# A hybrid encoder layer: the first norm's weight moved behind the transposes, all token tiles loaded first, some roots on ScalarE, the last token tile in two column halves

## The chip, the cores and the metric

The kernel runs on one core of a Trainium2 chip. The core has five engines with their own instruction streams: TensorE (PE; its weight loads are listed as PEld), VectorE (DVE), ScalarE (ACT), GpSimd (POOL) and SyncE (SP), which here issues the transfers between device memory and on-chip memory. Engines wait for each other by semaphores. Matrix products are written to PSUM, eight banks of 128 x 512 float32; everything else lives in SBUF, with 128 partitions. The metric is the time of one execution on the device in microseconds (us); lower is better.

## The reference, cut to what matters

One layer of an encoder trunk over 1024 tokens of width 1024, in float32. Each of its three sub-layers normalises its input, computes, normalises its output and adds it to the residual:

```python
def _rms_norm(x, gain):
    y = x * lax.rsqrt(jnp.mean(x * x, axis=-1, keepdims=True) + EPS)
    return y * gain

h = _rms_norm(x, g_mix_pre)
proj = h @ w_in                       # (1024, 1024) @ (1024, 2832)
...                                   # windowed attention and two-way gated DeltaNet
x = x + _rms_norm(mix @ w_out, g_mix_post)
...                                   # cross-attention into 256 memory tokens
x = x + _rms_norm(c, g_cross_post)
f = _swiglu(_rms_norm(x, g_ffn_pre), w_gate_up, w_down)
return x + _rms_norm(f, g_ffn_post)
```

The change touches the first norm (`g_mix_pre`) and the last one (`g_ffn_post`), at the two ends of the kernel.

## The kernel before, in words

Tokens go in eight tiles of 128 rows. A product in full precision is made of three products of rounded parts: each operand is split into a high part (a cast, usually on ScalarE, line 103) and a low part (the difference, usually on VectorE, line 104) by `split`, and `gemm_b` (line 260) issues high x high, high x low and low x high for each of the eight slices k of the inner dimension.

The instructions are written in Python and then placed by a planner: within each engine they are ordered by a priority, which follows the program's order, as its simulated clock makes them ready. `tc.high_priority(300)` in `load_w` moves weight loads and their splits 300 places up, and `tc.issue_after(i)` puts an instruction behind `i` on the same engine. Each engine then runs its stream strictly in that order. Buffers of one tag are reused in turn: an instruction that writes a buffer waits for the last reader of what was in it before. All transfers are issued by SyncE, in the planner's order too.

The start (lines 201 to 232). Six token tiles of `x` are loaded (line 205), and after the first of them `gmix`, the first norm's weight, which is spread to all 128 partitions (512 KB), and the identity matrix for transposes. Tiles 6 and 7 take over the buffers of tiles 0 and 1 (line 217). For each tile: ScalarE squares it and sums the squares (line 220), GpSimd makes the inverse root in two operations (`rstd_of`, lines 160 and 161), VectorE multiplies the tile by the root and by `gmix` in one operation (line 223), TensorE turns its eight 128 x 128 blocks into two PSUM tiles (line 228), and each of these is split into the high and low part of the turned activations `hT` (lines 103 and 104). Four tiles make a half `hf`. The first weights, two columns blocks of 128, are loaded behind tiles 1 and 3 (line 293), and their products with both halves follow (line 298): 96 matmuls of 128 x 512. Next come the products with `wabr` (line 314), a small weight that is zeroed (line 306) and filled (307, 308). In between, a small table of gains and convolution taps (`rows`) is turned (line 242), two masks are cast (246, 247), and `nega` is an exponential of a parameter (252).

The end (lines 1709 to 1783). The down projection of the feed-forward part is done by seven block products. The last of them runs over four token tiles t; for each, the activations come in two pieces of 6 and 5 slices (line 1763), are split, and 33 matmuls add to the PSUM tile X[t] (line 1768). After that, for token tile r = 4 + t: the sum `zv` (line 1775), its sum of squares on ScalarE (`sq_of`, line 1690), the gain `gp` (1777), the inverse root on GpSimd (`rstd_at`, lines 1705 and 1706), and for each column half the scaling together with the residual (1780) and the store (1781). The other half's sum of squares, in `sq[:, 1]`, has been made before the loop. `first_half` finishes tiles 2 and 3 within the same loop.

Of the kernel before, what the change touches and what calls it, by code (L numbers as in the profile page):

```python
# [76 lines left out]
def tile_hybrid_block(  # L77
# [16 lines left out]
    def f32(ap):  # L94
        return ap.bitcast(F32)
# [61 lines left out]
    def rstd_of(rs, ss, n, eps):  # L157

        w = ss.shape[-1]
        nc.gpsimd.tensor_scalar(rs, ss, n, eps, ALU.mult, ALU.add)  # L160
        nc.gpsimd.tensor_tensor(rs, rs, mhalf[:, :w], ALU.pow)


    gain_at = {"cross": 60, "mem": 60 + KT, "ffn": 60 + 2 * KT}
# [44 lines left out]
    hT = []  # L209
    for hf in range(2):  # L210
        hi = hx.tile([P, KT, HALF], F32R, name=f"hhi{hf}")
        lo = hx.tile([P, KT, HALF], F32R, name=f"hlo{hf}")
        for j in range(4):
            t = 4 * hf + j
            xt = xts[t] if t < 6 else t1.tile([P, D], F32, tag="xt", name="xt", bufs=6)
            if t >= 6:
                nc.sync.dma_start(xt, x[t * P:(t + 1) * P, :])
            junk = t1.tile([P, D], F32, tag="junk", name="junk", bufs=1)
            ss = t1.tile([P, 1], F32, tag="ss", name="ss", bufs=4)
            nc.scalar.activation(junk, xt, AF.Square, accum_out=ss)  # L220
            rs = t1.tile([P, 1], F32, tag="rs", name="rs", bufs=4)
            rstd_of(rs, ss, 1.0 / D, EPS)
            nc.vector.scalar_tensor_tensor(xt, xt, rs, gmix, ALU.mult, ALU.mult)
            for kq in range(2):
                pt = small()
                for k in range(4):
                    c = (4 * kq + k) * P
                    nc.tensor.transpose(pt[:, k * P:(k + 1) * P], xt[:, c:c + P], ident)
# [16 lines left out]
    nc.sync.dma_start(C, consts[:, C0:C1])  # L245
    nc.vector.tensor_copy(mU_r, cm["mU"])
    nc.vector.tensor_copy(mL_r, cm["mL"])
# [4 lines left out]
    nc.scalar.activation(nega, prm[:, 0:8], AF.Exp)  # L252
    nc.vector.tensor_scalar(nega, nega, -1.0, None, ALU.mult)
# [51 lines left out]
    wabr = tb.tile([P, KT, P], F32R, tag="V", name="wabr", bufs=1)  # L305
    nc.vector.tensor_scalar(wabr, hT[0][0].bitcast(F32)[:, :, 0:P], 0.0, None, ALU.mult)
    nc.vector.tensor_copy(wabr[:, :, 0:16], wab)
# [1380 lines left out]
    def sq_of(src, t, ch):  # L1688
        jk = tp_.tile([P, 512], F32, tag="jk", name="jk", bufs=1)
        nc.scalar.activation(jk, src, AF.Square, accum_out=sq[:, ch, t:t + 1])  # L1690

# [62 lines left out]
    for t in range(4):  # L1754
        nc.vector.tensor_tensor(za[:, t], za[:, t], X[t], ALU.add)
        sq_of(za[:, t], 4 + t, 1)

    for t in range(4):
        tt = slice(t * P, (t + 1) * P)
        for k0, n in ((0, 6), (6, 5)):  # L1760
            with tc.high_priority(AHEAD):
# [3 lines left out]
                split(ah, al, ar)  # L1765
            for k in range(n):
                for i, (a, w) in enumerate(((ah, t4h), (ah, t4l), (al, t4h))):
                    nc.tensor.matmul(X[t], a[:, k], w[:, k0 + k], start=False, stop=(k0 + k == NB - 1 and i == 2),  # L1768
                                     skip_group_check=True)
        if t < 2:  # L1770
# [3 lines left out]
        nc.vector.tensor_tensor(za[:, t], za[:, t], gp[:, 512:], ALU.mult)  # L1774
        nc.vector.tensor_tensor(zv[:, t], zv[:, t], X[t], ALU.add)
        sq_of(zv[:, t], r, 0)
        nc.vector.tensor_tensor(zv[:, t], zv[:, t], gp[:, 0:512], ALU.mult)
        rs = rstd_at(r)
        for z, o_ in ((za, 512), (zv, 0)):
            nc.vector.scalar_tensor_tensor(z[:, t], z[:, t], rs, xr[:, o_:o_ + 512], ALU.mult, ALU.add)  # L1780
            nc.sync.dma_start(out[there(r), o_:o_ + 512], z[:, t])
    LB.close()
# [31 lines left out]
```

## Time and profile before

| | |
|---|---|
| time, median of 3 runs | 1532.86 us (1529.66 to 1533.37) |
| the profiled execution's own time | 1531.94 us |
| its span, first to last instruction | 1530.2 us |
| TensorE busy | 1477.9 us, 97% of the span |
| VectorE, ScalarE, GpSimd busy | 1111.5, 743.0, 399.9 us |
| mean granted TensorE clock | 0.992 |
| HBM read and written | 179.41 MB, 75.27 MB |

The profile is one execution, recorded by the hardware profiler. A timeline row gives the start in us from the span's start, the duration in us, the engine, the line of the kernel (which can be a helper's), the operation, what it writes and reads by the program's names, and how many like it are merged (x8). In brackets stands the engine's idle time before it and what ended it. A row of the groups by line gives the count, then busy us and mean ns of one, then idle time and its releasers. A row of the stretches gives, for a stretch of time, its length and the busy time and number of instructions of PE, PEld, DVE, ACT and POOL, then the granted clock, the busy share of the DMA engines and GB/s. The chain of waits follows the work that ended last, from step to step, with start and duration; SPq, DVEq and the like are an engine's sequencer. Matmuls are pipelined: a recorded 0.39 us per matmul stands for a start every 0.23 us.

### The profile page before, as it was taken

The page shows a single profiled execution, that of the slowest core. Times are in us where ns is not written, and L with a number is a line of the kernel's source. Part 1 is how long each engine was busy: PE and PEld are TensorE (multiplying, and loading weights), DVE is VectorE, ACT ScalarE, POOL GpSimd, SP SyncE. Part 2 cuts the span into 40 slices and gives each one's busy share as a digit, 9 for nine tenths or more (in the row PEclk, how much of TensorE's full clock was granted, in tenths as well). Part 3 has the DMA queues.
Part 4 walks back from the last instruction along what each step waited for, and adds up shares of the span by engine and source line. Part 5 has one row for each costly group of instructions (what it writes and reads, how often), then busy time and mean ns, then how long its engine had stood idle before and what let it go on. Part 6 is the DMA issues. An engine that isn't in the chain of part 4 may idle for free.

```text
span 1530.2 us, 21184 instructions
## 1 busy us (share of the span) xinstructions
PE 1477.9 (97%) x7403; PEld 1241.1 (81%) x7403; DVE 1111.5 (73%) x1790; ACT 743.0 (49%) x1516; POOL 399.9 (26%) x404
## 2 busy tenths in 40 slices
PE   6999999998999899999999899999999999999997
PEld 5888888887989778887788687888888888888786
DVE  6868999787889865538567778686877554696665
ACT  5678821457557664455544673322233332454532
POOL 3020221311336203242201532353434332000021
PEclk9999999999999999999999999999999999999999
DMA  6235575857987674457724733343433333953255
GB/s 206 77 105 152 140 198 145 224 166 204 315 283 223 202 276 155 152 161 257 235 97 173 232 124 117 113 149 107 156 124 104 103 103 111 325 204 97 103 177 167
DMA packets 272360, 258.70 MB, mean 169 GB/s; under 512 B 34792, under 2 KB 204669, under 8 KB 272253
## 3 DMA queue, kind: packets, MB, share of 16 engines
q1 hardware_dynamic: 272253, 257.35, 53.4%
q8 instruction: 58, 0.95, 0.3%
q14 instruction: 49, 0.40, 0.1%
HBM read 179.41 MB, written 75.27 MB: 166 GB/s over the span
## 4 chain that ended last, share of the span: by engine, by line
PE 63%; DVE 10%; DMA 8%; ACT 4%; issue 3%; SPq 1%; POOL 1%; DVEq 0%; POOLq 0%; ACTq 0%
PE pE L1465 8%; PE pD L1465 8%; PE pA L1465 7%; PE pmg L1069 6%; PE pdX L1671 6%; PE pcq L260 4%; PE pdA L1671 4%; PE pB L1465 4%; PE pst L1285 3%; PE psc L808 2%; PE pdD L1671 2%; DMA wraw<-in_w_ckv_dram 1%; PE pg L260 1%; PE pdX L1768 1%; DMA kv<-d_kv 1%
## 5 line engine op out<-in xcount | busy, mean ns | idle before, releaser
L103 ACT CAST whi<-wraw 128x1024 fp32r<-128x1024 f32 x96 | 100.9, 1052 | 140.0 <-DMA wraw<-in_w_gate_up_dram 29.7
L104 POOL TENSOR_TENSOR wlo<-wraw,whi 128x1024 fp32r<-128x1024 f32 x38 | 92.3, 2428 | 197.4 <-ACT whi L103 197.3
L260 PE MATMUL pg<-hlo,whi 128*128 128x512 f32 x352 | 139.4, 396 | 0.0
L260 PE MATMUL pg<-hhi,whi 128*128 128x512 f32 x352 | 139.1, 396 | 0.0
L260 PE MATMUL pg<-hhi,wlo 128*128 128x512 f32 x352 | 138.1, 393 | 0.0
L1465 PE MATMUL pA<-b,whi 128*128 128x512 f32 x352 | 112.7, 400 | 5.0 <-ACT b L105 2.6
L104 DVE TENSOR_TENSOR wlo<-wraw,whi 128x1024 fp32r<-128x1024 f32 x58 | 73.5, 1269 | 40.7 <-ACT whi L103 38.2
L1465 PEld LDWEIGHTS pA<-b,whi 128*128 128x128 f32 x352 | 67.1, 192 | 19.5 <-ACT m L1492 3.0
L1671 PE MATMUL pdX<-dhl,whi 128*128 128x512 f32 x264 | 76.1, 390 | 1.5 <-DVE zv L1730 0.7
L260 PEld LDWEIGHTS pg<-hhi,whi 128*128 128x128 f32 x352 | 66.3, 189 | 13.4 <-ACT hhi L103 0.2
L260 PEld LDWEIGHTS pg<-hhi,wlo 128*128 128x128 f32 x352 | 66.3, 188 | 12.8
L260 PEld LDWEIGHTS pg<-hlo,whi 128*128 128x128 f32 x352 | 66.3, 188 | 12.7
L1548 POOL TENSOR_TENSOR act<-act,up 128x512 f32<-128x512 f32 x33 | 50.3, 1524 | 88.5 <-DVE up L1547 50.1
L1465 PE MATMUL pA<-b,wlo 128*128 128x512 f32 x176 | 69.8, 397 | 0.0
L103 ACT CAST whi<-araw 128x1024 fp32r<-128x1024 f32 (+1 forms) x36 | 35.3, 981 | 68.1 <-PE pdX L1671 27.6
L104 DVE TENSOR_TENSOR wlo<-araw,whi 128x1024 fp32r<-128x1024 f32 (+1 forms) x36 | 40.7, 1131 | 36.2 <-ACT whi L103 36.0
L1705 POOL TENSOR_SCALAR frs<-sq 128x1 f32<-128x1 f32 x8 | 12.0, 1498 | 194.5 <-ACT jk L1690 193.6
L285 DVE SCALAR_TENSOR_TENSOR acc<-cp,cols,acc 128x1024 f32<-128x1024 f32 x48 | 62.0, 1294 | 0.1
L1520 POOL TENSOR_TENSOR sr<-wraw 128x512 f32<-128x512 f32 x22 | 30.1, 1367 | 120.5 <-DMA wraw<-in_w_gate_up_dram 82.6
L1671 PEld LDWEIGHTS pdX<-dhl,whi 128*128 128x128 f32 x264 | 49.3, 188 | 12.7 <-issue 1.1
L103 ACT CAST dhl<-b 128x512 fp32r<-128x512 f32 x66 | 40.3, 619 | 31.4 <-PE pdA L1671 13.6
L1521 DVE TENSOR_TENSOR sr<-sr,wraw 128x512 f32<-128x512 f32 x22 | 36.1, 1639 | 25.5 <-POOL sr L1520 25.5
(481 smaller groups left out, 4326.0 us busy)
## 6 DMA issues: line engine op xcount, KB each, us to landing
wraw<-in_w_gate_up_dram SPq DMA_DIRECT2D x52, 512.0 KB, 3.9
kv<-d_kv SPq DMA_DIRECT2D x32, 512.0 KB, 7.1
wraw<-in_w_in_dram SPq DMA_DIRECT2D x22, 512.0 KB, 4.5
b<-in_w_down_dram SPq DMA_DIRECT2D x20, 512.0 KB, 7.7
araw<-d_as SPq DMA_DIRECT2D x20, 512.0 KB, 3.7
pz<-d_pz SPq DMA_DIRECT2D x32, 256.0 KB, 6.9
wraw<-in_w_ckv_dram SPq DMA_DIRECT2D x16, 512.0 KB, 5.2
wraw<-in_w_out_dram SPq DMA_DIRECT2D x16, 512.0 KB, 3.7
```

The costliest lines, as they stand in the source:

```text
L103: nc.scalar.copy(hi, src)
L104: return (eng or nc.vector).tensor_tensor(lo, src, f32(hi), ALU.subtract)
L260: nc.tensor.matmul(p_, w[:, k, :], ah[a][:, k, :], start=(k == 0 and i == 0), stop=(k == nk - 1 and i == 2))
L285: nc.vector.scalar_tensor_tensor(acc, cp[:, t:t + S], taps[t], acc, ALU.mult, ALU.add)
L808: nc.tensor.matmul(out[:, d, h, :], lt[:, d, h, :], rt[:, d, h, :], start=True, stop=True)
L1069: nc.tensor.matmul(pp[t], act[a][:, k, tt], w_[:, kk, :], start=(k == 0 and i == 0), stop=(k == KT - 1 and i == 2))
L1285: nc.tensor.matmul(bank, a[:, tt], w, start=(start and i == 0), stop=(stop and i == 2), skip_group_check=not check)
L1465: nc.tensor.matmul(out_, w[a][:, k, :], xx[b_][:, k, :], start=(start and k == 0 and i == 0), stop=(k == HK - 1 and i == 2), skip_group_ch ...
L1520: nc.gpsimd.tensor_tensor(s[0], b_[:, 0:HK], b_[:, HK:], ALU.add)
L1521: nc.vector.tensor_tensor(s[1], s[0], a_[:, 0:HK], ALU.subtract)
L1548: nc.gpsimd.tensor_tensor(o_, o_, up, ALU.mult)
L1671: nc.tensor.matmul(banks[t], a[:, k - k0, tt], w, start=(first and k == 0 and i == 0), stop=(k == NB - 1 and i == 2), skip_group_check=not ...
```

## The change

Four edits.

1. The first norm's weight is no longer spread over the partitions and multiplied into rows. It is loaded as eight rows of 128 (`grow`), turned once on TensorE into a column per slice (`gcol`), and multiplied in where the turned rows leave PSUM: the cast takes it as its scale, the difference as its factor. With this, a PSUM tile holds one slice k of four token tiles instead of four slices of one token tile; the transposes of a half come after its four tiles are scaled.
2. All eight token tiles are loaded into buffers of their own before anything else. The two first weight loads both go behind tile 3 on SyncE; their splits are placed on ScalarE and VectorE behind the fourth tile's root and scaling, and behind the cast and difference of slice 5.
3. The inverse roots of the first norm and of tiles 4 to 7 of the last one are a Sqrt on ScalarE and a reciprocal on VectorE (`inverse_root`) instead of two GpSimd operations. A Sqrt of a constant (`warm`) comes first. The masks, the zero fill of `wabr` and `nega` are put behind the last scaling or root.
4. In the last block product both pieces of the activations are fetched before the matmuls, and the last token tile is computed in two column halves of 256, the second into another PSUM bank (`XL`); sum, squares and gain are done for each half.

```diff
-    nc.gpsimd.memset(mhalf, -0.5)
+    nc.gpsimd.memset(mhalf[:, 0:8], -0.5)
+    epsc = mhalf[:, 8:9]
+    nc.gpsimd.memset(epsc, EPS)
...
+    def inverse_root(rs, ss, scale, bias):
+        root = nc.scalar.activation(rs, ss, AF.Sqrt, bias=bias, scale=scale)
+        nc.vector.reciprocal(rs, rs)
+        return root
...
-    xts = [t1.tile([P, D], F32, tag="xt", name="xt", bufs=6) for _ in range(6)]
-    gmix = t1.tile([P, D], F32, tag="gmix", name="gmix", bufs=1)
+    xts = [t1.tile([P, D], F32, tag="xt", name="xt", bufs=NT) for _ in range(NT)]
+    grow = t1.tile([KT, P], F32, tag="grow", name="grow", bufs=1)
+    gcol = t1.tile([P, KT], F32, tag="gcol", name="gcol", bufs=1)
     xload = []
-    for t in range(6):
+    for t in range(NT):
         xload.append(nc.sync.dma_start(xts[t], x[t * P:(t + 1) * P, :]))
         if t == 0:
-            nc.sync.dma_start(gmix, g_mix_pre[0].partition_broadcast(P))
+            nc.sync.dma_start(grow, g_mix_pre[0].rearrange("(c p) -> c p", p=P))
             nc.sync.dma_start(ident, consts[:, 0:P])
+    warm = t1.tile([P, 1], F32, tag="ss", name="warm", bufs=4)
+    nc.scalar.activation(warm, epsc, AF.Sqrt)
+    pt = small()
+    nc.tensor.transpose(pt[:, 0:KT], grow, ident[0:KT, 0:KT])
+    nc.vector.tensor_copy(gcol, pt[:, 0:KT])
...
             nc.scalar.activation(junk, xt, AF.Square, accum_out=ss)
             rs = t1.tile([P, 1], F32, tag="rs", name="rs", bufs=4)
-            rstd_of(rs, ss, 1.0 / D, EPS)
-            nc.vector.scalar_tensor_tensor(xt, xt, rs, gmix, ALU.mult, ALU.mult)
-            for kq in range(2):
-                pt = small()
-                for k in range(4):
-                    c = (4 * kq + k) * P
-                    nc.tensor.transpose(pt[:, k * P:(k + 1) * P], xt[:, c:c + P], ident)
-                o = slice(4 * kq, 4 * kq + 4), slice(j * P, (j + 1) * P)
-                split(hi[:, o[0], o[1]], lo[:, o[0], o[1]], pt.rearrange("p (k t) -> p k t", k=4))
+            rooted = inverse_root(rs, ss, 1.0 / D, epsc)
+            scaled = nc.vector.tensor_scalar(xt, xt, rs, None, ALU.mult)
+        if hf == 0:
+            ready.append((rooted, scaled))
+        for k in range(KT):
+            pt = small()
+            for j in range(4):
+                nc.tensor.transpose(pt[:, j * P:(j + 1) * P], xts[4 * hf + j][:, k * P:(k + 1) * P], ident)
+            g = gcol[:, k:k + 1]
+            cast = nc.scalar.activation(hi[:, k, :], pt, AF.Identity, scale=g)
+            cut = nc.vector.scalar_tensor_tensor(lo[:, k, :], pt, g, f32(hi[:, k, :]), ALU.mult, ALU.subtract)
+            if hf == 0 and k == 5:
+                ready.append((cast, cut))
...
-    ws = [load_w(dcols(1, h), KT, P, after=xload[t]) for h, t in ((0, 1), (1, 3))]
+    ws = []
+    for h in range(2):
+        with tc.issue_after(ready[h][0].ins), tc.issue_after(ready[h][1].ins):
+            ws.append(load_w(dcols(1, h), KT, P, after=xload[3]))
...
+    nc.vector.tensor_tensor(zv[:, 3, 256:], zv[:, 3, 256:], X[3][:, 256:], ALU.add)
+    XL = bank("pdY")
 
     for t in range(4):
         tt = slice(t * P, (t + 1) * P)
+        tiles = []
         for k0, n in ((0, 6), (6, 5)):
...
-            for k in range(n):
+            tiles += [(ah[:, k], al[:, k]) for k in range(n)]
+        columns = [(slice(0, 512), X[t])] if t < 3 else [(slice(0, 256), X[t][:, 0:256]), (slice(256, 512), XL[:, 0:256])]
+        for c_, p_ in columns:
+            fresh = c_.start > 0
+            for k, (ah, al) in enumerate(tiles):
                 for i, (a, w) in enumerate(((ah, t4h), (ah, t4l), (al, t4h))):
-                    nc.tensor.matmul(X[t], a[:, k], w[:, k0 + k], start=False, stop=(k0 + k == NB - 1 and i == 2),
-                                     skip_group_check=True)
+                    nc.tensor.matmul(p_, a, w[:, k, c_], start=(fresh and k == 0 and i == 0), stop=(k == NB - 1 and i == 2),
+                                     skip_group_check=not fresh)
...
-        nc.vector.tensor_tensor(zv[:, t], zv[:, t], X[t], ALU.add)
-        sq_of(zv[:, t], r, 0)
-        nc.vector.tensor_tensor(zv[:, t], zv[:, t], gp[:, 0:512], ALU.mult)
-        rs = rstd_at(r)
-        for z, o_ in ((za, 512), (zv, 0)):
-            nc.vector.scalar_tensor_tensor(z[:, t], z[:, t], rs, xr[:, o_:o_ + 512], ALU.mult, ALU.add)
-            nc.sync.dma_start(out[there(r), o_:o_ + 512], z[:, t])
+        known = sq[:, 1, r:r + 1]
+        nc.vector.tensor_scalar(known, known, D * EPS, None, ALU.add)
+        for c_, p_ in columns:
+            nc.vector.tensor_tensor(zv[:, t, c_], zv[:, t, c_], p_, ALU.add)
+            sq_of(zv[:, t, c_], r, 0)
+            nc.vector.tensor_tensor(zv[:, t, c_], zv[:, t, c_], gp[:, c_], ALU.mult)
+            if c_.stop < 512:
+                nc.vector.tensor_tensor(known, known, sq[:, 0, r:r + 1], ALU.add)
+        rs = tp_.tile([P, 1], F32, tag="frs", name="frs")
+        inverse_root(rs, sq[:, 0, r:r + 1], 1.0, known)
+        for z, o_, c_ in [(za, 512, slice(0, 512))] + [(zv, 0, c_) for c_, _ in columns]:
+            at = slice(o_ + c_.start, o_ + c_.stop)
+            nc.vector.scalar_tensor_tensor(z[:, t, c_], z[:, t, c_], rs, xr[:, at], ALU.mult, ALU.add)
+            nc.sync.dma_start(out[there(r), at], z[:, t, c_])
```

Left out of the diff: `with tc.issue_after(scaled.ins)` around the two mask casts and the zero fill of `wabr`, `with tc.issue_after(rooted.ins)` around `nega`, and the width of the scratch tile in `sq_of`.

More of the change, by code (lines that the diff above doesn't have):

```diff
@@ L213, in tile_hybrid_block @@
         for j in range(4):
[L214 to L217, printed above, removed]
+            xt = xts[4 * hf + j]
             junk = t1.tile([P, D], F32, tag="junk", name="junk", bufs=1)
@@ L245, in tile_hybrid_block @@
     nc.sync.dma_start(C, consts[:, C0:C1])
-    nc.vector.tensor_copy(mU_r, cm["mU"])
-    nc.vector.tensor_copy(mL_r, cm["mL"])
+    with tc.issue_after(scaled.ins):
+        nc.vector.tensor_copy(mU_r, cm["mU"])
+        nc.vector.tensor_copy(mL_r, cm["mL"])
     nc.sync.dma_start(prm[:, 0:8], a_log[0].rearrange("d h -> (d h)").partition_broadcast(P))
@@ L251, in tile_hybrid_block @@
     nc.sync.dma_start(prm[:, 16:24], attn_sink[0].partition_broadcast(P))
-    nc.scalar.activation(nega, prm[:, 0:8], AF.Exp)
+    with tc.issue_after(rooted.ins):
+        nc.scalar.activation(nega, prm[:, 0:8], AF.Exp)
     nc.vector.tensor_scalar(nega, nega, -1.0, None, ALU.mult)
@@ L305, in tile_hybrid_block @@
     wabr = tb.tile([P, KT, P], F32R, tag="V", name="wabr", bufs=1)
-    nc.vector.tensor_scalar(wabr, hT[0][0].bitcast(F32)[:, :, 0:P], 0.0, None, ALU.mult)
+    with tc.issue_after(scaled.ins):
+        nc.vector.tensor_scalar(wabr, hT[0][0].bitcast(F32)[:, :, 0:P], 0.0, None, ALU.mult)
     nc.vector.tensor_copy(wabr[:, :, 0:16], wab)
@@ L1689, in sq_of @@
         jk = tp_.tile([P, 512], F32, tag="jk", name="jk", bufs=1)
-        nc.scalar.activation(jk, src, AF.Square, accum_out=sq[:, ch, t:t + 1])
+        nc.scalar.activation(jk[:, 0:src.shape[-1]], src, AF.Square, accum_out=sq[:, ch, t:t + 1])
     def there(t):
```

2 lines of the change are left out of this document (1 added, 1 removed).

## Prediction

> **What bounds the kernel now.** I read the summary page first, then the busy time by stretch, then the timeline of the two ends that the change touches. The page:
>
> ```profile
> span 1530.2 us, 21184 instructions
> ...
> PE 1477.9 (97%) x7403; PEld 1241.1 (81%) x7403; DVE 1111.5 (73%) x1790; ACT 743.0 (49%) x1516; POOL 399.9 (26%) x404
> ...
> PE 63%; DVE 10%; DMA 8%; ACT 4%; issue 3%; SPq 1%; POOL 1%; DVEq 0%; POOLq 0%; ACTq 0%
> ```
>
> TensorE is busy 97% of the span and carries 63% of the chain that ended last. So a gain has to give TensorE its first large matmuls sooner, or shorten what follows its last one. The stretches (columns: PE, PEld, DVE, ACT, POOL busy; clock; DMA share; GB/s) show where it is not full:
>
> ```profile
> 0.00:20.00 20.00, 7.85 (x33) 6.46 (x34) 10.76 (x12) 13.49 (x22) 9.23 (x29) 1.00 0.92 298
> 20.00:40.00 20.00, 19.34 (x91) 15.96 (x92) 13.21 (x23) 10.45 (x20) 2.40 (x5) 1.00 0.38 99
> 40.00:60.00 20.00, 20.00 (x91) 16.32 (x90) 18.48 (x25) 9.33 (x13) 0.14 (x2) 1.00 0.23 67
> ...
> 380.00:400.00 20.00, 17.12 (x136) 16.06 (x135) 15.40 (x48) 8.38 (x19) 4.16 (x4) 1.00 0.95 330
> ```
>
> The first 20 us hold 12 us without TensorE work while the transfers run at 0.92. The timeline of that start:
>
> ```profile
> 4.39 1.06 ACT L220 ACTIVATE junk<-xt 128x1024 f32<-128x1024 f32 x1 [2.32 <-DMA xt<-in_x_dram]
> ...
> 6.70 1.28 DVE L223 SCALAR_TENSOR_TENSOR xt<-xt,rs,gmix 128x1024 f32<-128x1024 f32 x1 [6.70 <-DMA gmix<-in_g_mix_pre_dram]
> ...
> 8.23 1.06 ACT L220 ACTIVATE junk<-xt 128x1024 f32<-128x1024 f32 x1 [2.69 <-DMA xt<-in_x_dram]
> ...
> 21.58 4.00 PE L228 MATMUL ps<-ident,xt 128*128 128x128 f32 x16 [0.54 <-DVE xt L223]
> ...
> 25.24 0.68 PE L260 MATMUL pg<-hlo,whi 128*128 128x512 f32 x1
> ...
> 31.89 1.04 PE L228 MATMUL ps<-ident,xt 128*128 128x128 f32 x8
> ...
> 34.34 0.27 PE L242 MATMUL ps<-ident,rows 128*128 128x128 f32 x1
> ...
> 48.55 0.39 PE L260 MATMUL pg<-hhi,wlo 128*128 128x512 f32 x1
> 48.77 0.39 PE L314 MATMUL pg<-hhi,wabr 128*128 128x512 f32 x1
> ```
>
> The first norm waits for gmix (512 KB, loaded ahead of the second token tile), and that tile's square starts only at 8.23. From 25.24 TensorE runs without a gap to the next product (L314) at 48.77; matmuls start 0.22 to 0.23 us apart. Transposes take 4.00/16 = 0.25 us each before 25.24 and 1.04/8 = 0.13 after it, so about the first 4 us of unbroken work run at half pace.
>
> The end, from the chain of waits and SyncE's timeline:
>
> ```profile
> 1515.32 7.33 PE pdX L1768 x31
> 1522.66 0.02 issue
> 1522.68 0.70 DVE zv L1775
> ...
> 1523.46 0.63 ACT jk L1690
> ...
> 1524.28 0.79 POOL frs L1705
> ...
> 1525.12 0.61 POOLq L1809
> ...
> 1525.76 0.75 DVE za L1780
> ```
> ```profile
> 1527.20 0.33 SPq L1781 DMA_DIRECT2D out_dram<-zv  x1
> ```
>
> After the last matmul (1522.66) one token tile goes through add, square, two GpSimd operations and two scalings; its last store is issued 4.54 us later.
>
> **The start, worked out.** Removed: 8 two-input multiplies of 1.28, the gmix transfer, 16 GpSimd operations. Added: 8 Sqrt, 8 reciprocals, 8 scalings, and the weight inside the 16 casts and 16 differences. The prices:
>
> ```profile
> L926 DVE TENSOR_SCALAR mt<-mt,mrs 128x1024 f32<-128x1024 f32 x2 | 1.5, 754 | 1.2 <-POOL mrs L161 1.2
> L1167 DVE RECIPROCAL csum<-csum 128x2 f32<-128x2 f32 x16 | 2.5, 159 | 1.9 <-ACT cpr L1165 1.9
> L105 ACT ACTIVATE b<-ptn,cols 128x512 fp32r<-128x512 f32 x16 | 10.2, 681 | 3.8 <-PE ptn L1035 2.4 <-PE ptn L1420 1.4
> L106 DVE SCALAR_TENSOR_TENSOR b<-ptn,cols,b 128x512 fp32r<-128x512 f32 x16 | 11.3, 745 | 4.5 <-ACT b L105 4.5
> ```
> ```profile
> 9.93 1.04 ACT L103 CAST whi<-wraw 128x1024 fp32r<-128x1024 f32 x1
> ...
> 12.13 1.22 DVE L104 TENSOR_TENSOR wlo<-wraw,whi 128x1024 fp32r<-128x1024 f32 x1
> ...
> 22.58 0.19 ACT L252 ACTIVATE nega<-prm 128x8 f32<-128x8 f32 x1
> ```
> ```profile
> GB/s 0 41 246 385 266 243 383 331 357 391 397 355 307 367 410 377 247 362 189 309 54 9 109 313 391 355 279 109 15 0 0 0 0 16 0 33 174 47 68 6
> ```
>
> L105 and L106 do the same cast and difference out of PSUM with a per-partition gain, later in this kernel. No row has a Sqrt of one column; between 0.19 (nega) and twice that, I take 0.28, as it also reads a bias column. The last row is the DMA rate in each us of the first 40. Its sum puts the first tile (0.52 MB) at 3.6, and its square started at 4.39; the second (1.64 MB, with gmix and ident ahead) at 7.2 and 8.23. So a tile can be used 0.8 to 1.0 after its bytes have passed. With gmix gone and weights queued behind tile 3, tile 3 ends at 2.16 MB: 8.7 + 0.9 = 9.6.
>
> From there: square 1.06 + 0.1 for its sum (10.8), Sqrt (11.05), reciprocal (11.25), scaling 0.75 (12.05). The transposes of the first three tiles have run by then as far as the five PSUM buffers allow. The fourth tile's takes 0.25 (12.35), the cast 0.68 (13.1). VectorE splits the first weight ahead of the first difference, 12.1 to 13.3, then the difference 0.75: 14.05. From then the products have what they need; a cast each 0.6 and a difference each 0.67 keep up with three matmuls of 0.227 per k.
>
> TensorE then owes, up to L314: 96 matmuls x 0.227 = 21.8; 44 transposes x 0.13 = 5.7; the small-table transpose 0.3; and half of some 4 us at the slow pace, 2.0. Together 29.8, so L314 at 43.8 instead of 48.77: **5.0 us earlier**. Tiles 4 to 7 must be turned by about 28, when the first token half is used up; with both weights and all eight tiles 5.3 MB have passed by 17.6 in the rate row, so they land by 18.5, and ScalarE's work from 11 on (two weight casts 2.1, four squares and roots 5.6, sixteen casts 9.6) ends by 29, half a tile ahead of need. Bounds: a one-us-later landing and 2 us of gaps leave 2.0; half the slow phase gone and the weight split taken second give 6.5.
>
> Queues: on SyncE the weights move behind two more token tiles and tiles 6 and 7 ahead of the small tables; the constants land some us later, but TensorE first turns them at 34.34, and no product of this start needs them. On ScalarE nega waits for the last root; it is first read at 68.65, so it costs nothing here:
>
> ```profile
> 68.65 0.28 DVE L345 TENSOR_TENSOR G<-la,nega 128x64 f32<-128x64 f32 x1
> ```
> On VectorE the masks and the zero fill of wabr wait for the last scaling; behind them stands only wabr's own copy, whose product is L314. GpSimd loses its roots; nothing queues there. Eight buffers of xt instead of six plus gmix take the two reloads (L217) off: their second landed only at 27.79, with ScalarE idle 3.64 us.
>
> ```profile
> 27.79 1.06 ACT L220 ACTIVATE junk<-xt 128x1024 f32<-128x1024 f32 x1 [3.64 <-DMA xt<-in_x_dram]
> ```
>
> [...] A Sqrt brings another function table. In the trace a table load is 1.28 us, and squares run after loads made for Silu as well as beside Exp:
>
> ```profile
> 104.51 1.28 ACT L286 ACT_TABLE_LOAD   x1 [0.93 <-DVE acc L285]
> ...
> 107.35 0.28 ACT L450 ACTIVATE jk<-ps 128x128 f32<-128x128 f32 x1
> ```
>
> So a square seems to need no table of its own; I count one load ahead of the first tile (hidden behind its transfer, as now), one for nega's Exp at about 21, and one in the last stage, all with ScalarE idle beside them: 0 us. [...]
>
> **The end, worked out.** Now the last tile is two halves of 256 columns. Starts of such matmuls in this kernel:
>
> ```profile
> 384.70 0.29 PE L948 MATMUL pck<-mT,wlo 128*128 128x256 f32 x1
> ...
> 385.78 0.28 PE L948 MATMUL pck<-mT,wlo 128*128 128x256 f32 x1
> ```
>
> Nine starts lie from the first to the second row: 0.12 each. 66 x 0.12 = 7.9 against 33 x 0.227 = 7.5: TensorE ends 0.4 later. The first half's add, square and gain hide under the second. After the last matmul: add 0.42 (an add of 512 takes 0.70, less 256 elements at the rate above), square 0.42 + 0.1, Sqrt 0.28, reciprocal 0.16, the 512-wide scaling 0.75, two halves 0.4 each, with some 0.25 of handing over: the last store is issued at 3.2 instead of 4.54. Net **0.9 us** gained; bounds 0.2 and 1.6. The wait for the last tile's operand (L1768 restarts at 1515.32) may shift 0.6 either way and enters only the range.
>
> **Sum.** 5.0 + 0.9 = 5.9, against the profiled execution's own 1531.94 (span 1530.2): 1526.0. That execution lies 0.9 under the median of the three runs (1532.86, 1529.66 to 1533.37), so on that footing 1526.9. I give 1526.5. What lies between the two ends has unchanged code; TensorE is full in the 20 us from 40 that follow, so I let the early start pass through.
>
> **The rivals.** (1) The gain is lost on the way. The stage at 380 to 400 has TensorE at 17.1 of 20 with DMA at 0.95; a stage set by transfers starts with its own loads, and if those don't move up, the early start ends there: 1532 less the tail, 1531. For it: that row. Against: its loads are of data that earlier stages write, so they move with them. (2) ScalarE, in order, has squares of tiles 4 and 5 placed ahead of the first casts and stands until they land (14 to 15.5): the start is worth 1 to 2, 1530. For it: the present order already makes ScalarE stand 3.64 us for a tile (27.79). Against: the casts come earlier in program order and the weight cast fills the gap. (3) Slower: the new start shifts the order that the planner chooses for the DMA-bound stage, and one more transfer chain there opens. The chain's pieces there show its price:
>
> ```profile
> 379.39 7.43 DMA kv<-d_kv
> ...
> 386.89 9.21 DMA wraw<-in_w_ckv_dram
> ```
>
> One more of each, 16.6, against the gain of 5.9: 1543. It decides once a block load is queued behind a weight load that it overtook before. (4) Square and Sqrt need two tables: 2.56 more per tile. Eight tiles add 20 us to ScalarE, whose casts then end at 49 instead of 29; the last 24 products follow, L314 at 54 (5.6 late); the tail gains 0.9 and loses a load: 1539 on the median's footing.
>
> **How the numbers follow.** The forecast 0.64 (own range 1521 to 1528.2); rivals 1 and 2 together 0.22; rival 3 0.11; rival 4 0.03. A change under 0.3% (4.6 us, below 1528.3 being faster and above 1537.5 slower) is what a measurement can hardly tell from none. So the forecast is faster, rivals 1 and 2 are the same, rivals 3 and 4 slower: faster 0.64, same 0.22, slower 0.14. The range goes from the upper bounds of the gains (6.5 + 1.6 + 0.6, and what VectorE's 5 us of saved work may add: 1520) through rivals 1 and 2 to 1534.
>
> **What would show it.** Right: the second tile's square near 6.5, the fourth tile's scaling near 12, the products unbroken from about 14, L314 near 44, no table load between square and root, 0.12 between the last 66 matmuls, the last store about 3.2 after them. Wrong: ScalarE standing for a token tile with casts ready; L314 at 47 or later; L314 early, and the kv loads of 368 at the same time as now; alternating table loads; a pace above 0.14 for the half-width matmuls, which alone takes the tail's gain.

## The result and the profile after

The changed kernel takes 1539.68 us (median of 9 runs, 1535.96 to 1544.17) against 1532.86 for the kernel before (9 runs beside them): ratio 1.0053, 95% interval 1.0036 to 1.0069. It is slower by 7 to 8 us, where 6 us of gain were forecast. The page of the profiled execution (1539.43 us, mean granted clock 0.988):

```profile
span 1537.7 us, 21284 instructions
...
PE 1481.8 (96%) x7437; PEld 1245.8 (81%) x7437; DVE 1102.8 (72%) x1812; ACT 746.7 (49%) x1531; POOL 380.7 (25%) x381
...
PE 55%; DVE 5%; DMA 3%; issue 2%; ACT 1%; POOL 0%; SPq 0%; DVEq 0%; ACTq 0%
```

TensorE is busy for 3.9 us more than before (1477.9), at a mean granted clock of 0.988 instead of 0.992, and idle for 3.6 us more: the span, 7.5 us longer, grew by waits and by a lower clock. Both ends did gain. The timeline of the start (line numbers are those of the changed kernel: L230 is the square, L233 the scaling, L276 the products, L241 the cast of the turned rows, L334 the product with `wabr`, which was L314):

```profile
7.57 1.06 ACT L230 ACTIVATE junk<-xt 128x1024 f32<-128x1024 f32 x1 [1.62 <-DMA xt<-in_x_dram]
8.54 0.18 ACT L230 ACTIVATION_READ_ACCUMULATOR junk<-xt 128x1 f32 x1
8.75 0.29 ACT L167 ACTIVATE rs<-ss,mhalf 128x1 f32<-128x1 f32 x1
...
12.01 0.75 DVE L233 TENSOR_SCALAR xt<-xt,rs 128x1024 f32<-128x1024 f32 x1
...
13.33 3.00 ACT L241 ACTIVATE hhi<-ps,gcol 128x512 fp32r<-128x512 f32 x5 [0.20 <-PE ps L239]
...
14.07 0.80 PE L276 MATMUL pg<-hhi,whi 128*128 128x512 f32 x1
...
16.20 1.08 ACT L230 ACTIVATE junk<-xt 128x1024 f32<-128x1024 f32 x1
...
27.19 1.80 PE L239 MATMUL ps<-ident,xt 128*128 128x128 f32 x15
...
42.60 0.39 PE L334 MATMUL pg<-hhi,wabr 128*128 128x512 f32 x1
```

The product that stood at 48.77 starts at 42.60, 6.2 us earlier. The timeline of the end:

```profile
1531.20 0.28 PE L1795 MATMUL pdY<-t4h,wlo 128*128 128x256 f32 x1
...
1534.31 0.88 SPq L1815 DMA_DIRECT2D out_dram<-zv  x2
```

The last matmul ends at 1531.48 and 6.2 us of the span follow; before it was 7.5 (1530.2 less 1522.65, where the last matmuls of the chain of waits end). So the time was lost between the ends. The stretches of the middle, before:

```profile
220.00:240.00 20.00, 18.87 (x103) 15.70 (x102) 18.81 (x36) 3.04 (x7) 10.66 (x20) 1.00 0.96 205
...
360.00:380.00 20.00, 17.56 (x116) 14.88 (x114) 17.79 (x38) 17.09 (x36) 5.88 (x7) 1.00 0.95 266
...
500.00:520.00 20.00, 18.38 (x122) 15.90 (x123) 17.86 (x43) 11.30 (x38) 5.53 (x10) 1.00 0.38 111
520.00:540.00 20.00, 17.39 (x85) 13.59 (x83) 15.24 (x29) 15.57 (x34) 0.20 (x1) 0.94 0.99 345
540.00:560.00 20.00, 19.95 (x82) 15.95 (x83) 11.66 (x16) 10.78 (x13) 0.00 (x0) 0.89 0.77 247
```

and after (the row of 380 to 400 before is in the prediction):

```profile
20.00:40.00 20.00, 20.00 (x106) 16.75 (x105) 13.66 (x28) 15.20 (x29) 0.00 (x0) 1.00 0.30 78
40.00:60.00 20.00, 20.00 (x93) 16.10 (x92) 18.52 (x30) 11.23 (x16) 0.27 (x4) 1.00 0.40 115
...
220.00:240.00 20.00, 16.93 (x95) 14.05 (x95) 18.86 (x37) 3.32 (x9) 7.91 (x17) 1.00 0.77 185
...
260.00:280.00 20.00, 18.83 (x92) 15.81 (x93) 15.84 (x37) 7.06 (x16) 2.07 (x2) 0.91 0.74 218
...
300.00:320.00 20.00, 17.53 (x97) 15.31 (x96) 14.69 (x42) 7.93 (x23) 3.11 (x7) 0.91 0.51 136
...
360.00:380.00 20.00, 15.41 (x80) 12.47 (x79) 14.26 (x38) 14.80 (x35) 5.07 (x8) 0.83 1.00 321
380.00:400.00 20.00, 16.46 (x122) 15.87 (x121) 12.40 (x34) 9.46 (x21) 3.62 (x2) 0.91 1.01 261
...
500.00:520.00 20.00, 16.59 (x111) 14.06 (x110) 16.12 (x37) 13.44 (x41) 5.78 (x10) 1.00 0.38 110
520.00:540.00 20.00, 15.88 (x70) 12.84 (x69) 13.71 (x24) 15.03 (x25) 1.67 (x2) 0.91 0.98 343
540.00:560.00 20.00, 17.20 (x85) 13.62 (x84) 12.99 (x29) 10.00 (x21) 0.40 (x2) 1.00 0.51 171
```

In each of these stretches from 220 on TensorE is less busy than before, and in four of them, up to 400, the clock is lower on top; 260 to 280 and 300 to 320 had 20.00 and 19.64 before, at 1.00. Over the nine stretches from 220 to 400 its busy time fell from 171.1 to 163.7 us, and the clock, 1.00 in all nine before, took up to 8.8 us more (0.91, 0.91, 0.83 and 0.91 of 20 us each). Here run the block inverse of the delta rule (its last small steps and `levels`, which loads the stored small blocks again and joins them), the attention windows, and the two-way scan, in code that the change does not touch. Two kinds of its work moved, by the timelines, before:

```profile
184.30 1.99 DVE L547 TENSOR_TENSOR V<-A,bB 128x1024 f32<-128x1024 f32 x1
...
552.56 0.58 SPq L689 DMA_DIRECT2D d_mix<-ao  x1
```

and after:

```profile
193.55 2.09 DVE L567 TENSOR_TENSOR V<-A,bB 128x1024 f32<-128x1024 f32 x1
...
583.98 0.59 SPq L709 DMA_DIRECT2D d_mix<-ao  x1
```

The first row closes the first serial chain of the block inverse, 60 small VectorE operations that each read what the one before wrote. It began 2 us later than before (133.29, was 131.24) and ended 9 later, since VectorE's records between the two points hold 44 other operations of some 42 us in all, where they held 33 of some 33. The second row is the last store of an attention window, 31 us later. The scan, which shares TensorE with the windows, ended at about the same time (its last transposes start at 517.43, before 515.81), so several windows were left over with nothing beside them.

To see where a lead is lost, I summed TensorE's work up to a point of time: each recorded matmul counts with about its time from start to start at full clock (512 columns 0.227 us, 384 0.172, 256 0.12, 128 and fewer 0.115; the medians in the trace of before are 0.227, 0.176, 0.12 and 0.11). What the sum is ahead of that of before, in us:

```
until us                        40    60   200   220   300   400   560   1500
changed kernel                +6.2  +6.2  +7.2  +6.9  +1.5  -8.3  -9.2  -8.5
tail alone                    +0.0  +0.2  -0.2  -0.5  -1.6  -2.3  +2.7  +1.1
start alone                   +5.3  +5.3  +6.3  +6.0  -0.8  -8.0 -10.6 -10.3
new start, old order          +6.7  +0.1  +0.1  +0.1  -0.6  +0.3  +3.5  +5.6
old start, new order          -0.5  -0.2  +0.2   0.0  -4.6 -14.9 -15.7 -18.4
changed, old order from 60    +7.2  +7.4  +5.6  +4.9  +4.4  +4.1  +7.6  +7.2
```

The first row is the result in one line: 7 us ahead at 220, 15 lost from there to 400, then nearly constant. The others are executions of the runs below. The tail alone has the order of before up to the last stage; its row tells how far two executions of one order differ, up to some 3 us either way. Each row is one execution, and some lie off their run's median: that of the new start with the old order took 1526.35 us (median 1531.64, the fastest of twelve), that of the old order from 60 us 1523.65 (median 1526.18). Nor is "nearly constant" exact: from 400 to 560 the three executions in the old order gain 3 to 5 us on that of before, whose clock was 0.89 from 540 to 560, and the three in the new order lose 1 to 3.

### The profile page after: what moved, and what is told of

It is laid out like the page before. It is cut to its first block, busy times and chain, and to the rows that moved or that the text cites. A ratio compares the mean times of both kernels' runs of the same rounds, so it can differ in the third digit from the quotient of the medians.

```text
span 1537.7 us, 21284 instructions
## 1 busy us (share of the span) xinstructions
PE 1481.8 (96%) x7437; PEld 1245.8 (81%) x7437; DVE 1102.8 (72%) x1812; ACT 746.7 (49%) x1531; POOL 380.7 (25%) x381
## 4 chain that ended last, share of the span: by engine, by line
PE 55%; DVE 5%; DMA 3%; issue 2%; ACT 1%; POOL 0%; SPq 0%; DVEq 0%; ACTq 0%
PE pE L1485 8%; PE pD L1485 8%; PE pA L1485 7%; PE pmg L1089 6%; PE pdX L1691 6%; PE pB L1485 4%; PE pst L1305 3%; PE pcq L276 3%; PE pdA L1691 2%; PE pdD L1691 2%; PE pdX L1795 2%; DMA b<-in_w_down_dram 1%; PE pco L1204 1%; DMA wpart<-in_w_co_dram 1%; PE pcs L1178 1%
## 5 line engine op out<-in xcount | busy, mean ns | idle before, releaser
L276 PE MATMUL pg<-hlo,whi 128*128 128x512 f32 x352 | 141.2, 401 | 0.0
L276 PE MATMUL pg<-hhi,whi 128*128 128x512 f32 x352 | 140.2, 398 | 0.0
L276 PE MATMUL pg<-hhi,wlo 128*128 128x512 f32 x352 | 139.5, 396 | 0.0
L276 PEld LDWEIGHTS pg<-hhi,whi 128*128 128x128 f32 x352 | 67.0, 190 | 13.8 <-ACT hhi L241 0.3
L276 PEld LDWEIGHTS pg<-hlo,whi 128*128 128x128 f32 x352 | 67.2, 191 | 12.8
L276 PEld LDWEIGHTS pg<-hhi,wlo 128*128 128x128 f32 x352 | 67.1, 190 | 12.8
L1540 POOL TENSOR_TENSOR sr<-wraw 128x512 f32<-128x512 f32 x22 | 29.8, 1355 | 122.2 <-DMA wraw<-in_w_gate_up_dram 83.7
L1485 PE MATMUL pB<-s0h,s1h 128*128 128x512 f32 x176 | 54.7, 392 | 0.0
```

Of the source, the lines that this page charges most:

```text
L276: nc.tensor.matmul(p_, w[:, k, :], ah[a][:, k, :], start=(k == 0 and i == 0), stop=(k == nk - 1 and i == 2))
L1485: nc.tensor.matmul(out_, w[a][:, k, :], xx[b_][:, k, :], start=(start and k == 0 and i == 0), stop=(k == HK - 1 and i == 2), skip_group_ch ...
L1540: nc.gpsimd.tensor_tensor(s[0], b_[:, 0:HK], b_[:, HK:], ALU.add)
```

## The experiments

My theory after the traces: the new start makes the planner put the unchanged middle into another order, and that order costs the 15 us. Rivals: the new start itself costs them, by its buffers or its transfers, whatever the order; or the tail does. The first four runs cross the two: each start with each order. For this the order of every engine's instructions, from the load `wab` to the end, was read out of one kernel's program and imposed on the other by edges that fix the issue order alone and wait for nothing. The tail alone takes the diff from `sq_of` on, with `inverse_root`; the start alone takes the rest. In the traces the orders hold: matched by operation, tile names and shape, TensorE's last 7280 of some 7400 matmuls stand in one sequence in the kernel before and in the new start with the old order, and in one sequence in the start alone and in the old start with the new order. The edges:

```diff
+    for e, packed in _ORDER.items():
...
+        mine = [i for i in traced[at:] if str(i.engine).split(".")[-1] == e and type(i).__name__ not in _QUIET]
+        last = None
+        for k in order_:
+            if last is not None:
+                tc.add_manual_dep(mine[k], last.name, mybir.DependencyInfo(mybir.DependencyClass.NoSync, mybir.DependencyReason.DATA), reason="order")
+            last = mine[k]
...
+    pinned(tc, wab_load.ins)
```

**Tail alone.**

> Only the edit of the last token tile, the start as before; the order of all instructions ahead of the tail is the one of before. Theory (the loss sits between 200 and 560 us and comes from the order that the planner makes of the middle after the new start): 0.8 to 1.1 us faster than before, ratio 0.9993 to 0.9995, not to be told from no change. Rival (the column halves and the roots on ScalarE cost the time): about 7 us slower.

1532.36 us against 1531.73, ratio 1.0001 (0.9989 to 1.0013). The tail is not what costs; its forecast 0.9 us lies inside the interval and can't be told from nothing.

**Start alone.**

> Only the edits of the start, the tail as before; the order of the middle is the one of the changed kernel. Theory: 7.5 to 8.5 us slower than before (6 us gained by 40 us, 14 lost from 200 to 560), about 1541. Rival (the tail costs): 6 us faster than before.

1540.99 us, ratio 1.0060 (1.0046 to 1.0075): 9.2 us slower, slightly more than expected. The start edits carry the whole loss.

**New start, old order.**

> The new start as in the run before it, but every engine and every queue has its instructions from the load of the decay weights to the end in the order in which they stand in the kernel before; no instruction is added. Theory (order): 5 to 6.5 us faster than before, about 1527, and 13 to 14 us faster than the start alone; the windows' stores end near 547 instead of 584. Rival (the new start itself, by where its buffers lie or by transfers that now meet, costs the time): still 7 to 8 us slower than before.

1531.64 us, ratio 0.9998 (0.9985 to 1.0011): 9.3 us better than the start alone, but no gain over before; 5 to 6.5 were expected. The table shows why: no loss in the middle, but the lead of 6.7 at 40 is gone at 60. (That this execution ends 5.6 ahead is not the run's rule; it is the fastest of twelve.) The timeline of this run around it (line numbers are larger by 27 than in the changed kernel):

```profile
48.79 0.72 ACT L439 ACTIVATE sct<-ang,CE 128x512 f32<-128x512 f32 x1 [0.93 <-DVE ang L438]
...
49.94 1.98 ACT L130 CAST whi<-wraw 128x1024 fp32r<-128x1024 f32 x2
...
51.02 0.50 PE L303 MATMUL pg<-hhi,whi 128*128 128x512 f32 x1 [1.36 <-ACT whi L130]
51.36 0.40 PE L303 MATMUL pg<-hlo,whi 128*128 128x512 f32 x1
53.74 0.74 PE L303 MATMUL pg<-hhi,wlo 128*128 128x512 f32 x1 [1.98 <-DVE wlo L131]
```

In the old order the cast of the next weight block stands behind a sine on ScalarE that waits for an angle; with TensorE 6 us earlier, the cast is late. In the changed kernel's own order it stood at 42.57. The stretches of this run, 4 us each, show that the 3.3 us of standing cost about twice their length (the clock is the third number from the end):

```profile
48.00:52.00 4.00, 2.40 (x10) 1.35 (x8) 3.96 (x6) 3.21 (x5) 0.13 (x2) 1.00 0.00 0
52.00:56.00 4.00, 2.26 (x7) 1.43 (x8) 3.90 (x8) 1.83 (x3) 0.00 (x0) 0.73 0.28 77
56.00:60.00 4.00, 4.00 (x12) 3.16 (x12) 2.62 (x5) 1.24 (x2) 0.00 (x0) 0.50 0.68 176
60.00:64.00 4.00, 4.00 (x20) 3.00 (x19) 2.01 (x6) 0.93 (x3) 0.00 (x0) 0.92 0.91 275
```

**Old start, new order.**

> The reverse: the start and the tail of before, with the instructions from the load of the decay weights to the end in the order in which they stand with the new start. Theory (order): 10 to 16 us slower than before, about 1546, the windows' stores end near 585. Rival (the new start itself): no change.

1546.25 us, ratio 1.0094 (1.0073 to 1.0115): 14.4 us slower, with the old start and the old tail. The order alone makes a loss of this size, without the new start's buffers and transfers; the new start without the new order makes none. The rival that the start itself costs it has fallen.

**The roots alone.** The smallest of the start's edits, one line of the norm (and the constant it reads):

```diff
-            rstd_of(rs, ss, 1.0 / D, EPS)
+            inverse_root(rs, ss, 1.0 / D, epsc)
```

> The kernel before, with one edit: the roots of the first norm by ScalarE and a reciprocal on VectorE in place of GpSimd's powers. Nothing else of the start or the tail is changed. In its order of instructions the attention windows' score products stand on average 35 matmuls later and the scan's products 17 earlier than before, nearly as with the whole new start (46 and 22), though the start itself changes little. Theory (the order that the planner makes of the middle costs the time, whatever set it off): 6 to 14 us slower than before, about 1542. Rival (the new start's own work or placement costs it): within 2 us of before, and if the roots are quicker than the powers, up to 2 us faster.

1543.15 us, ratio 1.0070 (1.0055 to 1.0086): 10.7 us slower. At 40 us TensorE is 1.4 behind, and at 300 it is 8.9. The same closing operation of the chain, in this run's timeline:

```profile
199.55 2.13 DVE L554 TENSOR_TENSOR V<-A,bB 128x1024 f32<-128x1024 f32 x1
```

So eight roots of 128 numbers, moved to another engine in the first 33 us, suffice to set off another order and a loss. This run was not repeated with the old order; that its loss comes by the order is concluded from the two runs before it.

**The changed kernel with the old order from about 100 us.**

> The changed kernel, start and tail, with the order of before only from about 100 us on; the first 100 us stay in the planner's order. Theory: in the run with the old order from the decay weights on the lead of 6.5 us at 40 us was lost between 49.5 and 60, because there ScalarE's split of the next weight block stands behind the sine of an angle that VectorE finishes at 48.8, TensorE stands still for 3.3 us and its clock falls to 0.50; with the planner's order there the lead stays, and the middle loses nothing: 6 to 7.5 us faster than before, about 1525, windows' stores end near 547. Rival (an early start cannot pass through the stage at 360 to 440 us, which its transfers set): within 2 us of before.

1529.21 us against 1532.24, ratio 0.9977 (0.9963 to 0.9990): 3.5 us faster, half of what was expected. The lead stays to 100 (+5.1) and is +1.3 at 140: where the two plans meet, TensorE waits 1.41 us for an operand of VectorE's and 1.17 for one of ScalarE's, and the clock stays whole. These two waits are 2.6 of the 3.8 us.

**Windows planned ahead, in the changed kernel and in the one before.** One line around the body of `next_windows`:

```diff
+        with tc.high_priority(200):
```

> The changed kernel with one line more: the attention windows are planned 200 places ahead. In the order of instructions their score products then stand 1.6 matmuls later than before on average instead of 46, the scan's 0.5 earlier instead of 22. Theory: most of the 14 us come back, 4 to 8 us faster than before, about 1526; a part can stay lost, since single windows still stand up to 22 places off. Rival (start itself, or the stage's transfers): still 6 to 8 us slower than before.

1538.38 us, ratio 1.0032 (1.0018 to 1.0047): still 5 us slower, not 4 to 8 faster. To bring the windows back to their places is not enough.

> The control to the run before it: the kernel before with the windows planned 200 places ahead (score products 18 matmuls earlier than before on average, scan 10 later). Theory: the time follows how windows and scan stand to each other; with the windows earlier still than in before the gain over before is small or none, -4 to +4 us. If it is faster than before by as much as the run before it, then the priority is a gain of its own and says nothing of the start.

1538.10 us, ratio 1.0037 (1.0022 to 1.0053): the same line costs the kernel before 5.7 us, more than the 4 that were expected at most. One stream moved by hand did not mend one order and spoilt the other; which other stream it made late was not followed up.

**VectorE alone in the old order.** The same edges as above, for VectorE alone:

> The changed kernel, start and tail, with VectorE alone in the order of before (from about 100 us on); the other engines and the queue are planned anew around it. In the changed kernel the serial chain of 60 small operations of the block inverse (it ended 9.25 us later than before, 193.55 instead of 184.30, though it began only 2 us later) has 8 convolution and other operations more between its links. Theory (first place of the loss is this chain): with VectorE's old order it ends near 183, the block inverse's readers start earlier, and by the new plan the windows' products stand 11 matmuls later than before instead of 46: 0 to 6 us faster than before. Rival (the windows' own place is all that counts): a gain of no more than a quarter of the 14 us, 3 to 6 us slower than before.

1551.66 us against 1532.63, ratio 1.0124 (1.0110 to 1.0139). The chain ended at 180.19, as expected, but the time is the worst of all, 19 us over before. The engines that were planned anew around it lost some 27 us of TensorE's work between 300 and 420, in an execution that was the longest of four (1556.21). The expectation failed: an early chain, with the other engines planned anew, brings nothing.

**The old order from about 200 us.**

> The changed kernel with the old order of all engines only from about 200 us on. Up to 200 the changed kernel's trace had a lead of 7 us of TensorE's work, but the chain of the block inverse was 9 us late. Theory (the chain is late through the order before 200): the lead is lost between 215 and 300 all the same, where TensorE waits for what comes from the chain, and the result lies within 3 us of before, not 6 faster. Rival (only the order of the windows and of the scan from 200 to 560 costs): 6 to 7 us faster than before.

1537.28 us, ratio 1.0029 (1.0018 to 1.0040): 4.4 us slower, which neither side expected. TensorE stands 11.6 us at 205 to 217 for a convolution that is late where the two plans meet, and the lead goes from +8.3 at 200 to -5.1 at 220. Behind that nothing more is lost (-4.6 at 400), although the chain ended only at 192.49. So the old order from 200 on carried a late chain without further loss; but TensorE itself was late by then, so the run does not decide between the two.

**Windows planned ahead, and VectorE in the old order to the end of the first chain.** Both edits together:

> The changed kernel with the windows planned 200 places ahead, as in an earlier run, and VectorE in the order of before from 100 us to the end of the first chain of the block inverse. Theory: chain near 183, the lead of 6 us not lost at 215 to 280, so 3 to 7 us better than with the windows' priority alone, about 1533, or faster than before if the windows, which now stand 17 matmuls earlier than before, cost nothing by that. Rival (the chain does not matter): the same as with the windows' priority alone, 5 us slower than before.

1529.54 us, ratio 0.9979 (0.9966 to 0.9992): 3.2 us faster than before, and 8 better than with the windows' line alone (1.0032). So VectorE's order between 100 and 190, with what the planner builds on it, carries a good part of the loss; the windows' place alone does not. The execution that was profiled took 1537.0, the longest of twelve, so I don't read from its trace where the time went.

**The changed kernel with the old order from about 60 us.** As from 100, with the edges set in earlier:

> The changed kernel with the old order of all engines from about 60 us on, so that the weight splits near 40 and 45 us stay where the planner put them for the new start, and no change of plan falls into the decays and key products at 100 to 120, where the run with the old order from 100 us on lost 3 to 4 us. Theory: the lead of 5 to 6 us is still there at 120 and, with the old order, is partly kept: 3 to 6.5 us faster than before, about 1528, and 0 to 4 us faster than with the old order from 100 on. Rival (the chain of the block inverse, which begins when its loads are in and not when TensorE is early, sets the levels' start, and so no lead passes 200 to 240 whatever the order): within 1.5 us of the run with the old order from 100 on, some 3 us faster than before, the lead of TensorE's work under 2 us at 240.

1526.18 us against 1532.68, ratio 0.9971 (0.9953 to 0.9988): 4.4 us faster by the ratio, the lowest of all, though its interval overlaps those of the two other runs that gained (0.9977 and 0.9979), so that the step from 100 to 60 us is not shown to be a gain. The stretches of this run:

```profile
380.00:400.00 20.00, 18.93 (x153) 17.95 (x152) 15.46 (x45) 11.12 (x28) 5.36 (x5) 1.00 1.04 348
...
520.00:540.00 20.00, 17.10 (x79) 13.09 (x78) 16.34 (x30) 14.06 (x26) 0.20 (x1) 0.91 0.95 346
540.00:560.00 20.00, 19.83 (x87) 15.89 (x86) 10.62 (x9) 10.83 (x12) 0.00 (x0) 1.00 0.85 282
```

and its timeline:

```profile
178.87 1.98 DVE L594 TENSOR_TENSOR V<-A,bB 128x1024 f32<-128x1024 f32 x1
...
546.31 0.59 SPq L736 DMA_DIRECT2D d_mix<-ao  x1
```

The chain closes 5.4 us earlier than before, the last window's store 6.25 earlier, and the table shows the lead from 40 us to the end. With the order kept, the early start passes through every stage of this execution, the one at 380 to 400 with its DMA share of 1.04 among them (+4.4 at 300, +4.1 at 400).

## Why the prediction was wrong

The step that failed is the one between the ends: "What lies between the two ends has unchanged code; TensorE is full in the 20 us from 40 that follow, so I let the early start pass through." Unchanged code is not an unchanged order. The planner orders instructions as its simulated clock makes them ready, as told with the kernel before, and the start is the first thing on that clock. The crossed runs put numbers on the step: the new order costs 9.3 us with the new start (1540.99 against 1531.64) and 14.5 with the old (1546.25 against 1531.73). With the old order held from 60 us on, the same edits gain 4.4 us (1.8 to 7.2 by the interval), and the 5.9 that were summed lie within that.

**The start, forecast 5.0.** The mechanism was right, and L314's successor came 6.2 earlier. The second square was forecast too early (7.57, forecast 6.5), and ScalarE then took the tiles one behind the other: the fourth scaling starts at 12.01, where the sum had it end at 12.05. That the first product still stands at 14.07 (14.05) is luck in part, since it needs the cast alone and the sum had made it wait for the difference too. The Sqrt took 0.29 (0.28). From 14.07 to 42.60 TensorE needed 28.5 us, for which 29.8 were summed; that is where the 1.2 lie. Two terms were too large: transposes start 0.11 us apart in the row at 27.19 (0.13 summed, 44 times), and the slow pace, summed with 4 us, lasted only some 2.6 behind 14.07, to about 16.7 (a matmul's record takes 0.78 us at 15.87 and 0.39 at 16.80). No table load stands between square and root (the second tile's sum ends at 8.72, its root starts at 8.75), and ScalarE makes five casts before the fifth tile's square (16.20). Rivals 2 (ScalarE blocked) and 4 (two tables) are excluded by these rows.

**The tail, forecast 0.9.** Right by the trace: 1.3 us less behind the last matmul, of which the half-width matmuls at 0.12 give back 0.4 by the prediction's sum. The timed runs of the tail alone can't separate it from zero.

**Rival 1, gain lost in the stage of 380 to 400.** For it spoke that stage's DMA share (0.95 before). The last run speaks against it: TensorE is 18.93 busy there, more than before, at a DMA share of 1.04, and its lead goes from 4.4 at 300 to 4.1 at 400.

**Rival 3, the planner's order, chance 0.11.** Its cause was the right one, and its place was half right. I priced it as one more chain of a block load and a weight load in the stage at 380 to 400 (DMA share 0.95 before), 16.6 us. Of the 15 us that are lost, about half go from 220 to 360, where VectorE's operations, the windows and the scan stand to each other in another way, and about half from 360, where TensorE's work is 1.2 behind, to 400, where it is 8.3. There TensorE's longest wait is for the cast of the first weight block of `w_ckv`. Its load was issued at 377.57, behind six `kv` loads (365.61 to 371.89); before it stood at 367.48, behind two (363.87 and 366.26), and the product at 379.00 did not wait:

```profile
387.17 1.04 ACT L103 CAST whi<-wraw 128x1024 fp32r<-128x1024 f32 x1 [4.25 <-DMA wraw<-in_w_ckv_dram]
...
388.27 0.51 PE L968 MATMUL pck<-mT,whi 128*128 128x256 f32 x2 [3.54 <-ACT whi L103]
```

The two crossed runs in the new order show the same wait (3.66 us in the start alone, 2.68 in the old start with the new order); the new start with the old order has none. So this rival was nearer than its chance says; that 16.6 lies close to 15 is luck, since the load came late and no whole chain was added. The profile of before could have carried a higher chance: VectorE was busy 53.6 of the 60 us from 130 to 190, beside the chain, so other work put between its links would make it late.

**What stays open.** Which pairs of instructions in the new order cost how much. The chain of the block inverse was late in every run that lost more than 7 us except one (VectorE alone, 180.19), so its lateness is a sign and was not shown to be the price; with the old order from 200 us on it was late and nothing more was lost from 220 to 400. `levels` begins to read the inverse only at 214.82 in the changed kernel (217.52 before), long after it was stored, so something else holds those loads; what, wasn't tried. Nor was it settled why the planner's clock changes its mind over eight roots.

## What to carry to other kernels

Where a planner orders the instructions, an edit's price is the edit plus the new order of everything behind it; here some 6 us gained against 15 lost in the middle. Before a gain at the start is let through, compare the two orders of the unchanged part, engine by engine, which needs no run; and where they differ, measure the edit with the old order held fast, beginning soon behind the edit. Moving one stream back by a priority (5.7 us lost in the kernel before), or one engine by its old order (19 us), can cost more than it repairs.

## What the runs showed of the hardware

In these traces a standstill of TensorE of 2.4 to 3.5 us cost between nothing and its own length again. In the run with the new start and the old order, 3.3 us of standing at 49.7 to 53.7, with two matmuls in between, were followed by a granted clock of 0.73, 0.50 and 0.92 in the next three stretches of 4 us: 1.1 + 2.0 + 0.3, another 3.4 us; the two make the 6.6 us that the table loses from 40 to 60. The changed kernel's stretches show the same at 365: 3.1 us of standing, and 0.83 and 0.50 in two stretches of 5 us, 3.4 us. The 3.54 us before 388.27 cost 1.6 more (0.60 in 388 to 392). And a gap of 2.53 us (before 222.75) left the clock alone (1.00 in 220 to 224 and in 224 to 228), while in the start alone the gap before the same transposes, 2.44 us (before 223.69), was followed by 0.57 in 224 to 228, 1.7 us. The changed kernel, and in the last two rows the start alone:

```profile
220.00:224.00 4.00, 1.30 (x10) 0.85 (x9) 3.85 (x8) 0.00 (x0) 3.53 (x7) 1.00 1.00 254
365.00:370.00 5.00, 1.88 (x5) 0.95 (x5) 2.94 (x8) 4.82 (x13) 1.37 (x3) 0.83 0.92 244
370.00:375.00 5.00, 5.00 (x20) 4.68 (x21) 3.26 (x9) 0.99 (x2) 0.77 (x2) 0.50 1.02 390
388.00:392.00 4.00, 3.73 (x19) 3.73 (x20) 1.13 (x4) 2.30 (x5) 2.35 (x1) 0.60 1.01 317
```
```profile
220.00:224.00 4.00, 1.56 (x9) 1.02 (x8) 3.86 (x9) 0.00 (x0) 3.70 (x8) 1.00 1.06 248
224.00:228.00 4.00, 3.92 (x17) 3.04 (x16) 3.79 (x9) 0.00 (x0) 0.78 (x2) 0.57 1.04 265
```

The clock of a whole stretch went down to half (0.50) here, and not below. In 365 to 370 five matmuls ran, and it fell all the same; of two gaps of about 2.5 us it fell behind one (2.44) and not behind the other (2.53). What decides was not settled. So the 15 us of lost work hold only some 7.4 us of standing (171.1 less 163.7), the rest being pace (the lower clock, up to 8.8), and the standstills above, 2.4 to 3.5 us long, cost from once to about twice their length.

A load of ScalarE's table took 1.28 us, and the next function ran 0.02 us behind it. In the timeline of the changed kernel, with the last root ending at 24.18:

```profile
24.20 1.28 ACT L268 ACT_TABLE_LOAD   x1
25.50 0.21 ACT L268 ACTIVATE nega<-prm 128x8 f32<-128x8 f32 x1
```
